# Stick-breaking attention with keys swept upwards: the factor of the later key blocks is applied after the value product, and the scores are computed four steps ahead

## The chip, the cores and the metric

The kernel runs on one core of one Trainium2 chip. The metric is the device time of one execution in microseconds (us), lower is better. The engines are named as the profile names them: PE is TensorE's matrix multiply and PEld its weight load, DVE is VectorE, ACT is ScalarE, POOL is GpSimd, SP is SyncE, which issues most transfers. Each engine runs its own instructions in the order in which the program gives them, and waits on semaphores for the others.

## The reference

A two-layer decoder trunk of width 1024 over 1024 tokens, all in float32. The part that the change touches is the stick-breaking attention of the first layer: eight heads of width 64, strictly causal.

```
def block(args):                       # one block of 128 queries
    z = jnp.einsum('bhqd,bhkd->bhqk', q_i, k) * scale
    mask = kpos[None, :] < qpos[:, None]
    log_fail = jnp.where(mask, jax.nn.log_sigmoid(-z), 0.0)
    later = lax.cumsum(log_fail, axis=3, reverse=True) - log_fail
    a = jnp.where(mask, jnp.exp(jax.nn.log_sigmoid(z) + later), 0.0)
    return jnp.einsum('bhqk,bhkd->bhqd', a, v)
```

So a key's weight is sigmoid(z) times the product of (1 - sigmoid(z)) over the keys between it and the query: each weight needs a sum over all *later* keys of the row. With sp = softplus(z) = max(z,0) + ln(1+exp(-|z|)), the weight is exp(z - sum of sp over this key and the later ones).

## The kernel before

The whole trunk is one program. Its stages follow each other: the first layer's projections with the gated delta rule, then stick-breaking attention, then the output projection, feed-forward, and the second layer. The time is spent above all in matrix products in which each float32 factor is split into two parts of the format fp32r ("hi" and "lo") and three of the four partial products are formed (`mm3`, lines 156 to 158).

Stick-breaking is the stretch of the program from line 899 to line 1066, and only it and the preparation of its operands are touched. The eight heads are taken as four pairs (`p` = 0 to 3). Within a pair a *step* is one block of 128 keys (`kb`) against one block of 256 queries (`i`), both heads of the pair at once, so most tiles are 128 keys by 2x256 queries, written 128x512. A pair has 20 steps, the four pairs 80. Two query blocks are always interleaved, (3, then 0) with (2, then 1). In 4 of a pair's 20 steps the key block reaches beyond half of the queries; such a half step works on the second half alone (128x2x128, which the profile writes 128x256). Before the change the keys of a query block run downwards, from the last block to block 0.

The pipeline of a step has these pieces, each a letter of the string `SORDER`, which sets the order in which the loop over n (line 1025) issues them; `Z+3` means "piece Z of step n+3", and because the loop is recorded by hand (`manual_schedule`), the engines run exactly this order:

- Z, lines 918 to 921, PE: the scores z = k·q, the key in parts kh and kl, plus a mask matmul of 128 columns where the block meets the diagonal. Two PSUM banks for z.
- A, E, L, lines 926, 929 and 932, ACT: ab = ln(1+exp(-|z|)) in three activations.
- K, line 936, DVE: a copy ls of z from PSUM to SBUF, which sets z's bank free.
- M, line 939, DVE: ab = max(ls,0) + ab, the softplus.
- h, line 945, DVE, and l, line 948, POOL: ab is split into sh and sl.
- Q, lines 959 and 960, PE: the negated sum over the keys of this block that are not earlier (`nstr` holds minus ones in a triangle) is added into a bank `Pb` that lives through all steps of the query block.
- W, line 963, DVE: ls = ls + Pb. X, line 1022, ACT: ls = exp(ls), the finished weights.
- C, lines 971 and 972, PE: the rest of the triangle (`ncom`) is added, so that Pb then holds the sum over the whole block for the blocks that follow. Left out in the last step of a query block.
- V, line 981, PE: weights times values, a plain float32 product, accumulated over the steps in the bank `av`, which ACT copies to `ob` (line 983) after the last step.

Three tokens bring in other work: `p` advances the preparation of the next pair's q and k (`prep_qk`: loads, a cast on ACT, a subtraction on POOL; `PREPS` says in which of the 20 steps which half of which operand starts), and `f` fills PE with matmuls that have nothing to do with the step: up to step 8 the last value projection (`v_gen`), and from step 18 on 64 units of three matmuls of the output projection (`out_gen`, lines 156 to 158, tile `ops`), about one unit a step. Every fourth unit needs an evacuation on DVE (line 304, below also "evac"), every sixteenth a new weight tile: a cast `whi` on ACT (line 141) and a subtraction `wlo` on DVE (line 142). In steps 13, 15, 17 and 19 the loop also splits four tiles of the delta rule's output into `o` (cast on ACT, line 1037, subtraction on DVE, line 1038), ahead of the step's own pieces. `VSHARE`, `OSPLIT`, `OSTART` and the rest of these numbers are the same in both kernels, and so is every instruction outside the stretch but for line numbers and the load of the constants `scr`.

Of the kernel before, what the change touches and what calls it, by code (L numbers as in the profile page):

```python
# [10 lines left out]
F32 = mybir.dt.float32  # L11
F32R = mybir.dt.float32r
AF = mybir.ActivationFunctionType
# [10 lines left out]
PREPS = {3: (0, 1), 6: (1, 1), 10: (0, 0), 15: (1, 0)}  # L24
SORDER = "Z+3 V-4 f Q+0 A+3 W+0 K+3 X-1 E+3 p p h+2 L+3 f C-1 l+2 M+3".split()
LSB, ABB, SHB = 8, 4, 3
# [35 lines left out]
def tile_trunk(ctx: ExitStack, tc: tile.TileContext, xT, cT, adaS, adaT, vec, w_ab, w_hyb, w_hout, w_rin, w_rout,  # L62
# [460 lines left out]
    def stack(tag, nm, p, half):  # L523
        i = 2 * p + 1 - half
        return (sqs[0] if i % 3 else sb0).tile([P, HT], F32R, tag=tag, name=nm, bufs=2 if i % 3 else 1)

    def prep_qk(p, isq, half, new, dma=None):

        src = qk_d[2 * p + isq][:, half * HT:half * HT + HT]
        dma = dma or nc.sync.dma_start  # L530
        if not isq:
            xs_ = []
            for h in range(2):
                x = new()
                for r in range(2):
                    dma(x[r * 64:r * 64 + 64], src[h * 64:h * 64 + 64])
                xs_.append(x)
            yield
            for h in range(2):
                kh = stacks[p, "kh", h, half] = stack(f"kh{h}", f"kh{p}{h}", p, half)  # L540
                kl = stacks[p, "kl", h, half] = stack(f"kl{h}", f"kl{p}{h}", p, half)
                A.copy(kh, xs_[h])
                yield
                G.tensor_tensor(kl, xs_[h], kh.bitcast(F32), op=ALU.subtract)
                yield
            return
        x = new()
        dma(x, src)
        yield
        ts = []  # L550
        for h in range(2):
            o = slice(h * 64, h * 64 + 64)
            qs = stacks[p, "q", h, half] = stack(f"q{h}", f"q{p}{h}", p, half)
            A.copy(qs[o], x[o])
            ts.append(qs)
            yield
        for h in range(2):
            o = slice(h * 64, h * 64 + 64)
            r = slice(64 - h * 64, 128 - h * 64)
            G.tensor_tensor(ts[h][r], x[o], ts[h].bitcast(F32)[o], op=ALU.subtract)  # L560
            yield

    def s_first():

        scr = sb0.tile([P, 4, P], F32R, tag="scr", name="scr")
        G.dma_start(scr[:, 0:3, :], cst[:, C_NSTR:C_NSTR + 3, :])
        V.tensor_copy(scr[:, 3, :], ident)
        scrs.append(scr)
        for isq in range(2):
            for _ in prep_qk(0, isq, 1, half_tile):  # L570
                pass
# [326 lines left out]
    with ExitStack() as sx:  # L898
        pz = sx.enter_context(tc.tile_pool(name="pz", bufs=2, space=PSUM))
        pP = sx.enter_context(tc.tile_pool(name="pP", bufs=1, space=PSUM))  # L900
        pav = sx.enter_context(tc.tile_pool(name="pav", bufs=1, space=PSUM))
        steps = []
        for p in range(4):
            two = [[dict(p=p, i=i, kb=kb, x=x, first=(kb == 2 * i + 1), last=(kb == 0), c0=128 if kb == 2 * i + 1 else 0)
                    for i in ii for kb in range(2 * i + 1, -1, -1)] for x, ii in enumerate(((3, 0), (2, 1)))]
            for pair in zip(*two):
                steps.extend(pair)
        cur = {}
        fin = []
# [13 lines left out]

        def stage_a(s):
            s["ab"] = ab = sp_.tile([P, HT], F32, tag="ab", name="ab", bufs=ABB).rearrange("p (h n) -> p h n", h=2)[:, :, s["c0"]:]
            A.activation(ab, s["z"], AF.Abs)
# [7 lines left out]
        def stage_k(s):  # L934
            s["ls"] = ls = sp_.tile([P, HT], F32, tag="ls", name="ls", bufs=LSB).rearrange("p (h n) -> p h n", h=2)[:, :, s["c0"]:]
            V.tensor_copy(ls, s["z"])

        def stage_sp(s):
            V.scalar_tensor_tensor(s["ab"], s["ls"], 0.0, s["ab"], op0=ALU.max, op1=ALU.add)

        def stage_hi(s):
            c0 = s["c0"]
            s["sh"] = sp_.tile([P, 2, 256], F32R, tag="sh", name="sh", bufs=SHB)[:, :, c0:]
            s["sl"] = sp_.tile([P, 2, 256], F32R, tag="sl", name="sl", bufs=SHB)[:, :, c0:]
            V.tensor_copy(s["sh"], s["ab"])
# [4 lines left out]
        def stage_h(s):  # L950
            stage_hi(s)
            stage_lo(s)

        def stage_t1(s):
            c0 = s["c0"]
            if s["first"]:
                cur["P", s["x"]] = pP.tile([P, 2, 256], F32, tag=f"P{s['x']}", name="Pb")
            s["P"] = Pc = cur["P", s["x"]][:, :, c0:]
            PE.matmul(Pc, nstr, s["sh"], start=s["first"], stop=False, skip_group_check=True)
            PE.matmul(Pc, nstr, s["sl"], start=False, stop=True, skip_group_check=True)  # L960

        def stage_t2(s):
            V.tensor_tensor(s["ls"], s["ls"], s["P"], op=ALU.add)

        def stage_t(s):
            stage_t1(s)
            stage_t2(s)

        def stage_c(s):
            if not s["last"]:  # L970
                PE.matmul(s["P"], ncom, s["sh"], start=False, stop=False, skip_group_check=True)
                PE.matmul(s["P"], ncom, s["sl"], start=False, stop=True, skip_group_check=True)

        def stage_av(s):
            p, i, kb, c0 = s["p"], s["i"], s["kb"], s["c0"]
            if s["first"]:
                cur["av", s["x"]] = pav.tile([P, 256], F32, tag=f"av{s['x']}", name="av")
            av = cur["av", s["x"]]
            for h in range(2):
                o = slice(h * 64, h * 64 + 64)  # L980
                PE.matmul(av[o, c0:], vts[p][:, kb, o], s["ls"][:, h, :], start=s["first"], stop=True, skip_group_check=True)
            if s["last"]:
                fin.append(lambda: A.copy(obt[p][:, i * 256:i * 256 + 256], av))
# [5 lines left out]
        nstr, ncom, negm, idr = (scrs[0][:, i, :] for i in range(4))  # L989
# [8 lines left out]
        with tc.manual_schedule(engines=COMPUTE):  # L998
# [3 lines left out]
            prep = [prep_qk(0, 0, 0, new_x, QD(nc)), prep_qk(0, 1, 0, new_x, QD(nc))]  # L1002
# [18 lines left out]
            def stage_x(s):  # L1021
                A.activation(s["ls"], s["ls"], AF.Exp)
            ops = dict(Z=stage_z, A=stage_a, E=stage_e, L=stage_l, K=stage_k, H=stage_h, T=stage_t, X=stage_x, C=stage_c, V=stage_av)
            ops.update(M=stage_sp, h=stage_hi, l=stage_lo, Q=stage_t1, W=stage_t2)
            for n in range(-6, 88):
# [22 lines left out]
                for f in fin:  # L1048
                    f()
                fin.clear()  # L1050
# [12 lines left out]
            for f in fin:  # L1063
                f()
# [830 lines left out]
```

## Time and profile before

| what | us |
|---|---|
| median of 3 runs | 3126.43 (3126.11 to 3132.8) |
| the profiled execution | 3130.16 |
| its span, first to last instruction | 3128.4 |
| granted TensorE clock, mean over the span | 0.991 |
| first softplus piece L of the stage (line 932) starts at | 620.5 |
| last of them starts at | 843.2 |
| last X of the stage (line 1022) starts at | 850.6 |
| first matmul of the output projection that reads `ob` | 854.64 |

The views used below are the windows (busy time of each engine in a stretch, with the mean granted TensorE clock and the share of the DMA engines), the groups (busy time and mean nanoseconds of one instruction for each line, engine and shape, and what ended the idle time ahead of them) and the timeline (start, duration, engine, line; in brackets how long the engine had been idle and who released it). A matmul's record is longer than the slot it takes, because matmuls overlap in the array: what a matmul costs PE is read from the start of one to the start of the next.

### The profile page before, as it was taken

The numbers are of one execution on the slowest core, as the hardware profiler recorded it, in microseconds if no ns is written. First come the engines' busy times: TensorE is split into PE (matmuls) and PEld (weight loads), VectorE is DVE, ScalarE is ACT, GpSimd is POOL, SyncE is SP. The second block draws the span as 40 slices with busy tenths as digits, with TensorE's granted clock in tenths as the row PEclk, the third lists the DMA queues.
The fourth block names the chain that finished last, engine by engine and source line by source line (L and its number), as shares of the span: only waits on it lengthen the run. The fifth ranks groups of instructions, "written<-read, shape, count | busy, mean of one in ns | idle before, by whom it ended". The sixth has DMA issues, their size and how long they took to land.

```text
span 3128.4 us, 38622 instructions
## 1 busy us (share of the span) xinstructions
PE 3008.5 (96%) x14616; PEld 2418.5 (77%) x14616; DVE 2118.7 (68%) x3065; ACT 1244.5 (40%) x2011; POOL 460.6 (15%) x332
## 2 busy tenths in 40 slices
PE   6999999999999999999999999999999899999999
PEld 3777788867677888887878788887777688888887
DVE  5778876599877655588582455578866976656445
ACT  4444556688763322221263332333223632223111
POOL 0233332077531000000040000001111300000000
PEclk8999999999999999999999999999999999999999
DMA  5333332241034322287125333362312342224222
GB/s 210 129 109 102 121 112 79 96 148 48 21 103 146 105 81 81 83 318 276 60 88 157 109 115 111 109 236 98 110 48 68 125 150 90 81 81 169 88 75 101
DMA packets 136602, 362.35 MB, mean 116 GB/s; under 512 B 15072, under 2 KB 24032, under 8 KB 135904
## 3 DMA queue, kind: packets, MB, share of 16 engines
q1 hardware_dynamic: 135808, 358.90, 34.3%
q8 instruction: 115, 1.88, 0.3%
q10 hardware_dynamic: 464, 0.79, 0.1%
q14 instruction: 71, 0.58, 0.1%
q0 software_dynamic: 144, 0.20, 0.0%
HBM read 282.76 MB, written 77.07 MB: 115 GB/s over the span
## 4 chain that ended last, share of the span: by engine, by line
PE 43%; DVE 8%; DMA 3%; issue 1%; ACT 1%; SPq 0%; DVEq 0%; ACTq 0%
PE ops L156 5%; PE ops L157 5%; PE ops L158 5%; PE rvps L1570 3%; PE mB L1271 2%; PE mB L1269 2%; PE mB L1270 2%; PE mD L1270 2%; PE mD L1269 2%; PE mD L1271 2%; PE mA L1269 2%; PE mA L1271 2%; PE mA L1270 2%; DMA adaw<-in_adaT_dram 1%; PE mE L1269 1%
## 5 line engine op out<-in xcount | busy, mean ns | idle before, releaser
L304 DVE SCALAR_TENSOR_TENSOR x<-ops,mod,x 128x512 f32<-128x512 f32 x288 | 215.3, 748 | 215.6 <-PE ops L158 215.1
L141 ACT CAST whi<-raw 128x1024 fp32r<-128x1024 f32 x158 | 165.5, 1051 | 398.7 <-PE ops L157 306.3
L156 PE MATMUL ops<-hdh,whi 128*128 128x512 f32 x704 | 276.4, 393 | 6.7 <-DVE x L304 6.3
L142 DVE TENSOR_TENSOR wlo<-raw,whi 128x1024 fp32r<-128x1024 f32 x158 | 208.1, 1319 | 101.1 <-ACT whi L141 96.5
L157 PE MATMUL ops<-hdl,whi 128*128 128x512 f32 x704 | 274.6, 390 | 0.0
L158 PE MATMUL ops<-hdh,wlo 128*128 128x512 f32 x704 | 274.1, 389 | 0.0
L156 PE MATMUL gps<-hh,whi 128*128 128x512 f32 x352 | 166.1, 472 | 0.0
L156 PEld LDWEIGHTS ops<-hdh,whi 128*128 128x128 f32 x704 | 132.1, 188 | 42.3 <-DVE x L304 12.3
L158 PEld LDWEIGHTS ops<-hdh,wlo 128*128 128x128 f32 x704 | 132.2, 188 | 27.9 <-issue 0.2
L157 PEld LDWEIGHTS ops<-hdl,whi 128*128 128x128 f32 x704 | 132.2, 188 | 26.9 <-issue 0.2
L192 POOL TENSOR_TENSOR nscr<-nscr 128x512 f32<-128x512 f32 x30 | 46.2, 1541 | 691.5 <-ACT nscr L191 633.6
L1261 ACT CAST thi<-raw 128x512 fp32r<-128x512 f32 x180 | 101.8, 618 | 114.4 <-DVE raw L1257 68.9
L157 PE MATMUL gps<-hl,whi 128*128 128x512 f32 x352 | 140.8, 400 | 0.0
L158 PE MATMUL gps<-hh,wlo 128*128 128x512 f32 x352 | 139.7, 397 | 0.0
L156 PE MATMUL ops<-osh,whi 128*128 128x512 f32 x320 | 128.3, 406 | 10.1 <-DVE x L304 8.1
L948 POOL TENSOR_TENSOR sl<-ab,sh 128x512 fp32r<-128x512 f32 (+1 forms) x80 | 116.4, 1455 | 140.6 <-ACT ab L932 73.8
L157 PE MATMUL ops<-osl,whi 128*128 128x512 f32 x320 | 128.1, 401 | 5.3 <-DVE osl L1749 4.8
L158 PE MATMUL ops<-osh,wlo 128*128 128x512 f32 x320 | 126.1, 395 | 0.0
L1262 DVE TENSOR_TENSOR tlo<-raw,thi 128x512 fp32r<-128x512 f32 x180 | 119.3, 710 | 3.3 <-ACT thi L1261 3.3
L1400 ACT ACTIVATE u<-u 128x512 f32<-128x512 f32 x44 | 27.8, 632 | 231.1 <-DVE u L1331 231.1
L1331 DVE TENSOR_TENSOR u<-u,mE 128x512 f32<-128x512 f32 x60 | 41.3, 688 | 112.2 <-PE mE L1271 112.2
L1311 DVE TENSOR_TENSOR u<-u,mB 128x512 f32<-128x512 f32 x60 | 41.3, 688 | 111.6 <-issue 100.1
(425 smaller groups left out, 8445.1 us busy)
## 6 DMA issues: line engine op xcount, KB each, us to landing
raw<-in_w_fin_dram SPq DMA_DIRECT2D x102, 512.0 KB, 3.8
raw<-in_w_rin_dram SPq DMA_DIRECT2D x64, 512.0 KB, 4.0
raw<-in_w_fout_dram SPq DMA_DIRECT2D x52, 512.0 KB, 3.6
adaw<-in_adaT_dram SPq DMA_DIRECT2D x48, 512.0 KB, 4.9
oraw<-hid_d SPq DMA_DIRECT2D x44, 512.0 KB, 5.3
gth<-in_adaT_dram SPq DMA_DIRECT2D x64, 256.0 KB, 2.8
raw<-in_w_hyb_dram SPq DMA_DIRECT2D x28, 512.0 KB, 3.6
hid_d<-c SPq DMA_DIRECT2D x44, 256.0 KB, 2.0
```

The source lines that it names most:

```text
L141: A.copy(hi, raw)
L142: V.tensor_tensor(lo, raw, hi.bitcast(F32), op=ALU.subtract)
L156: PE.matmul(ps, whi, xh, start=start, stop=False)
L157: PE.matmul(ps, whi, xl, start=False, stop=False)
L158: PE.matmul(ps, wlo, xh, start=False, stop=stop)
L304: V.scalar_tensor_tensor(xs[dt][:, sl], ps, gts(dt), xs[dt][:, sl], op0=ALU.mult, op1=ALU.add)
L948: G.tensor_tensor(s["sl"], s["ab"], s["sh"].bitcast(F32), op=ALU.subtract)
L1261: A.copy(hi, t)
L1262: e.tensor_tensor(lo, t, f32(hi), op=ALU.subtract)
L1269: PE.matmul(ps, w[0][:, c], xh[k], start=(start and k == 0), stop=False, skip_group_check=True)
L1270: PE.matmul(ps, w[0][:, c], xl[k], start=False, stop=False, skip_group_check=True)
L1271: PE.matmul(ps, w[1][:, c], xh[k], start=False, stop=(k == 3), skip_group_check=True)
```

## The change

The keys of a query block now run upwards, from block 0 to the diagonal. A step forms weights that hold only the sum over its *own* block, multiplies them with the values at once, and the result of the earlier steps is multiplied by the factor of the new block, because this block's keys are all later than theirs: acc = acc * exp(-sum of sp over this block) + weights·v. The accumulator is now `ob` in SBUF instead of a PSUM bank.

- Z moves to the end of the step and one step further ahead (`Z+4`), and z keeps its PSUM bank until X has read it; there are four banks for z.
- A of a full step is now a bit operation on DVE that clears the sign (line 930, from PSUM); only half steps keep ACT's Abs.
- K is gone; M reads z from PSUM.
- Q adds the triangle onto z itself, so W is gone, and X reads z in PSUM.
- C is replaced by S: four matmuls with a matrix of ones (`som`) that lay the sums of sp over the block, for both heads, into the second half of the new bank `av` (two banks, taken in turn), left out in the first step of a query block instead of the last.
- G is new, on ACT: g = exp(-sum), 128 partitions by 256 queries. R is new, on POOL: acc = acc * g. O is new, on DVE: acc = acc + av, or a copy in the first step. The four copies of `av` for each pair on ACT are gone.
- V runs one step behind instead of four.
- PREPS changes which halves are prepared when, and `stack` chooses the buffers accordingly; `scr` has three constants instead of four and is loaded by two transfers instead of one.

```
-SORDER = "Z+3 V-4 f Q+0 A+3 W+0 K+3 X-1 E+3 p p h+2 L+3 f C-1 l+2 M+3".split()
-LSB, ABB, SHB = 8, 4, 3
+PREPS = {3: (0, 0), 6: (1, 1), 15: (1, 0), 18: (0, 1)}
+SORDER = "A+3 Q+0 S+0 X+0 V-1 M+2 E+3 f h+2 R-1 L+3 p G+0 f l+2 O-1 Z+4 p".split()
+WB, ABB, SHB = 3, 4, 3
...
-        pz = sx.enter_context(tc.tile_pool(name="pz", bufs=2, space=PSUM))
-        pP = sx.enter_context(tc.tile_pool(name="pP", bufs=1, space=PSUM))
-        pav = sx.enter_context(tc.tile_pool(name="pav", bufs=1, space=PSUM))
+        pz = sx.enter_context(tc.tile_pool(name="pz", bufs=4, space=PSUM))
+        pav = sx.enter_context(tc.tile_pool(name="pav", bufs=2, space=PSUM))
...
+            if s["c0"]:
+                A.activation(ab, s["z"], AF.Abs)
+            else:
+                V.tensor_scalar(ab.bitcast(I32), s["z"].bitcast(I32), 0x7FFFFFFF, None, op0=ALU.bitwise_and)
...
-        def stage_k(s):
-            s["ls"] = ls = sp_.tile([P, HT], F32, tag="ls", name="ls", bufs=LSB).rearrange("p (h n) -> p h n", h=2)[:, :, s["c0"]:]
-            V.tensor_copy(ls, s["z"])
...
-            V.scalar_tensor_tensor(s["ab"], s["ls"], 0.0, s["ab"], op0=ALU.max, op1=ALU.add)
+            V.scalar_tensor_tensor(s["ab"], s["z"], 0.0, s["ab"], op0=ALU.max, op1=ALU.add)
...
-            V.tensor_tensor(s["ls"], s["ls"], s["P"], op=ALU.add)
...
+        def stage_q(s):
+
+            PE.matmul(s["z"], nstr, s["sh"], start=False, stop=False, skip_group_check=True)
+            PE.matmul(s["z"], nstr, s["sl"], start=False, stop=True, skip_group_check=True)
+
+        def stage_x(s):
+            s["w"] = half2(sp_.tile([P, HT], F32, tag="w", name="w", bufs=WB), s)
+            A.activation(s["w"], s["z"], AF.Exp)
+
+        def stage_s(s):
+
+            s["av"] = av = pav.tile([P, 2, 256], F32, tag="av", name="av")
             if s["first"]:
+                return
+            for h in range(2):
+                e = som[:, 64 - 64 * h:192 - 64 * h]
+                for j, t in enumerate((s["sh"], s["sl"])):
+                    PE.matmul(av[:, 1, s["c0"]:], e, t[:, h, :], start=(h + j == 0), stop=(h + j == 2), skip_group_check=True)
+
+        def stage_g(s):
+            if not s["first"]:
+                s["g"] = g = sp_.tile([P, 256], F32, tag="g", name="g", bufs=3)
+                A.activation(g[:, s["c0"]:], s["av"][:, 1, s["c0"]:], AF.Exp, scale=-1.0)
...
+                PE.matmul(s["av"][o, 0, c0:], vts[p][:, kb, o], s["w"][:, h, :], start=True, stop=True, skip_group_check=True)
...
+            if not s["first"]:
+                G.tensor_tensor(acc(s), acc(s), s["g"][:, s["c0"]:], op=ALU.mult)
+
+        def stage_o(s):
+            av = s["av"][:, 0, s["c0"]:]
+            if s["first"]:
+                V.tensor_copy(acc(s), av)
+            else:
+                V.tensor_tensor(acc(s), acc(s), av, op=ALU.add)
```

Two places show what the string makes of the engines' orders. A row names the line, the operation, the written tile and the read ones, and in brackets the engines whose semaphores it waits for.

The first is PE in a full step of the steady part of the stage. Before, the step begins with Q (lines 959, 960), then come C of the step ahead of it, Z, V and a unit of `f`:

```order
L959 MATMUL Pb<-sh,scr 128x512 [waits DVE_49]
L960 MATMUL Pb<-sl,scr 128x512 [waits Pool_49]
L971 MATMUL Pb<-sh,scr 128x512 [waits DVE_49]
L972 MATMUL Pb<-sl,scr 128x512
L918 MATMUL z<-q_5767,kh_5917 128x256 [waits DVE_49,PE_49]
L919 MATMUL z<-q_5767,kl_5918 128x256
L918 MATMUL z<-q_5805,kh_5945 128x256
L919 MATMUL z<-q_5805,kl_5946 128x256
L981 MATMUL av<-ls,vt_5659 64x128 [waits Activation_49]
L981 MATMUL av<-ls,vt_5659 64x128
```

The same place now, with Q (951, 952), S (966), V of the step before (977), the unit of `f`, and Z (917 on):

```order
L951 MATMUL z<-sh,scr 128x512
L952 MATMUL z<-sl,scr 128x512 [waits Pool_49]
L966 MATMUL av<-sh,som 128x256 [waits DVE_49]
L966 MATMUL av<-sl,som 128x256
L966 MATMUL av<-sh,som 128x256
L966 MATMUL av<-sl,som 128x256
L977 MATMUL av<-w,vt_6398 64x256 [waits Activation_49]
L977 MATMUL av<-w,vt_6398 64x256
L157 MATMUL ops<-o_6147,whi 128x512
L158 MATMUL ops<-o_6148,whi 128x512
L159 MATMUL ops<-o_6147,wlo 128x512
L917 MATMUL z<-q_6507,kh_6923 128x256 [waits Activation_49]
```

The wait that C had on DVE (W of the step before must have read Pb) has become S's wait on DVE: its bank `av` is the one that O of two steps before reads, and O of two steps before stands in DVE's order one loop step earlier, as the last of that step. Z's wait on DVE has become a wait on ACT (X of the same loop step).

The second place is DVE in a step in which a weight tile of the output projection is split (`wlo`). Before, `wlo` and the evacuation (line 304) stand at the start of the step, ahead of W, K, h and M:

```order
L939 SCALAR_TENSOR_TENSOR ab<-ls,ab 128x512 [waits DVE_49,Activation_49]
L142 TENSOR_TENSOR wlo<-raw,whi 128x1024 [waits DMAHW0_49,Activation_49]
L304 SCALAR_TENSOR_TENSOR x_5880<-ops,mod,x_5880 128x512
L963 TENSOR_TENSOR ls<-ls,Pb 128x512 [waits PE_49]
L936 COPY ls<-z 128x2x128 [waits Activation_49]
```

Now they stand inside the step, behind A (930) and M (940), ahead of h (944) and O (991):

```order
L930 TENSOR_SCALAR ab<-z 128x512 [waits PE_49]
L940 SCALAR_TENSOR_TENSOR ab<-z,ab 128x512 [waits Activation_49]
L143 TENSOR_TENSOR wlo<-raw,whi 128x1024 [waits DMAHW5_49,Activation_49]
L305 SCALAR_TENSOR_TENSOR x_5917<-ops,mod,x_5917 128x512
L944 CAST sh<-ab 128x512 [waits DVE_49]
L991 TENSOR_TENSOR ob_5321<-ob_5321,av 128x256 [waits PE_49,Pool_49]
```

A's wait on PE is for Z, the last piece of the PE step before, and `wlo`'s wait on ACT is for the cast `whi`, which now stands on ACT behind X and E of the same step. What is queued behind `wlo` is h and O, and S of the next step waits for O.

More of the change, by code (lines that the diff above doesn't have):

```diff
@@ L521, in load_v, with stack @@
         nc.sync.dma_start(vts[p], v_d[:, :, p * P:p * P + P])
[L523 to L524 removed]
+    def stack(tag, nm, p, half, isq):
+        i = 2 * p + (1 - half if isq else half)
         return (sqs[0] if i % 3 else sb0).tile([P, HT], F32R, tag=tag, name=nm, bufs=2 if i % 3 else 1)
@@ L988, in tile_trunk @@
         sp_ = sx.enter_context(tc.tile_pool(name="sbp", bufs=2, side="right"))
-        nstr, ncom, negm, idr = (scrs[0][:, i, :] for i in range(4))
+        nstr, negm, idr = (scrs[0][:, i, :] for i in range(3))
+        som = sp_.tile([P, 192], F32R, tag="som", name="som", bufs=1)
+        for i in range(3):
+            V.tensor_scalar(som[:, 64 * i:64 * i + 64], ones[:, 0:64], float(i == 1), None, op0=ALU.mult)
         xs = []
```

73 lines of the change are left out of this document (21 added, 52 removed).

## The prediction, made before the changed kernel was run

> **What bounds the kernel now.** I read the page first, then the windows over the stage, then the timeline of one steady step, and the groups for the prices. The page:
>
> ```profile
> PE 3008.5 (96%) x14616; PEld 2418.5 (77%) x14616; DVE 2118.7 (68%) x3065; ACT 1244.5 (40%) x2011; POOL 460.6 (15%) x332
> ```
>
> PE is busy nearly always, but that is an average over all stages, so it is read again for the stage alone (columns: window, its us, busy time and instructions of PE, PEld, DVE, ACT and POOL, the granted clock, the DMA share, GB/s).
>
> ```profile
> 656.60:695.30 38.70, 33.47 (x183) 22.66 (x182) 38.06 (x60) 34.12 (x68) 23.77 (x18) 0.96 0.40 133
> 695.30:849.20 153.90, 152.38 (x849) 110.34 (x848) 144.68 (x238) 127.85 (x248) 103.82 (x72) 1.00 0.12 37
> 849.20:855.90 6.70, 4.76 (x27) 2.51 (x26) 3.94 (x5) 4.68 (x7) 0.00 (x0) 0.99 0.13 27
> 852.00:855.70 3.70, 1.96 (x14) 0.85 (x10) 2.87 (x3) 3.44 (x6) 0.00 (x0) 1.00 0.20 32
> 855.70:859.10 3.40, 3.20 (x8) 2.53 (x9) 3.40 (x4) 1.73 (x2) 0.00 (x0) 0.51 0.31 124
> ```
>
> The first window is steps 10 to 22, in which the `o` splits stand, the second the steady steps 23 to 78, the third the tail from the last Q to the second matmul of the next stage. In the second PE and DVE both look full, 152.4 and 144.7 of 153.9 us. Which of the two sets the pace is read from starts:
>
> ```profile
> 706.35 0.40 PE L959 MATMUL Pb<-sh,scr 128*128 128x512 f32 x1
> ...
> 706.82 0.40 PE L971 MATMUL Pb<-sh,scr 128*128 128x512 f32 x1
> ...
> 707.29 0.28 PE L918 MATMUL z<-q,kh 128*128 128x256 f32 x1
> ...
> 707.85 0.65 PE L981 MATMUL av<-ls,vt 128*64 128x256 f32 x4
> 708.43 0.50 PE L156 MATMUL ops<-o,whi 128*128 128x512 f32 x1
> ...
> 709.23 0.40 PE L959 MATMUL Pb<-sh,scr 128*128 128x512 f32 x1
> ```
>
> Start to start, Q takes 0.47 us, C 0.47, Z 0.56, V 0.58, a unit of f 0.80: 2.88 us a step without a gap. PE's slots bound the steady stage, and DVE, 94% busy, is a near second. Where PE does wait, it is at `wlo`:
>
> ```profile
> 725.90 2.31 DVE L142 TENSOR_TENSOR wlo<-raw,whi 128x1024 fp32r<-128x1024 f32 x1
> 729.32 0.39 PE L960 MATMUL Pb<-sl,scr 128*128 128x512 f32 x1
> ...
> 730.22 0.36 PE L918 MATMUL z<-q,kh 128*128 128x256 f32 x1 [0.50 <-DVE ls L936]
> ```
>
> 730.22 is Z kept 0.50 us by K. The 153.9 us hold some 1.7 us of such waits in all: where `wlo` delays DVE by 2.31 us, PE loses about half a microsecond, since W, K and M then work a step or more ahead of what PE needs.
>
> **The change part by part: PE's slots.** Q, Z, V and f stay. S in a full step is four matmuls of 256 columns, C two of 512: 0.47 us either way. In a half step C's two take
>
> ```profile
> 726.73 0.28 PE L971 MATMUL Pb<-sh,scr 128*128 128x256 f32 x1
> 726.85 0.29 PE L972 MATMUL Pb<-sl,scr 128*128 128x256 f32 x1
> ```
>
> 0.12 us each by starts, 0.24 together; S's four of 128 columns lie between half of that each (0.24, nothing lost) and the same 0.12 each (0.48): 0 to +0.24 us. No row shows four such ones; I take +0.2, near the upper end, since four weight loads stay four. Twelve half steps lie outside the first window: **+2.4 us**. V one step behind instead of four only moves three V (3 x 0.58 = 1.7) from behind the last Q to before it: **+1.7**, which the tail gives back.
>
> **DVE's prices.** Groups of the steady window (busy us, mean ns, idle before):
>
> ```profile
> L939 DVE SCALAR_TENSOR_TENSOR ab<-ls,ab 128x512 f32<-128x512 f32 x45 | 39.8, 885 | 0.8 <-ACT ab L932 0.7
> L963 DVE TENSOR_TENSOR ls<-ls,Pb 128x512 f32<-128x512 f32 x46 | 31.3, 681 | 6.7 <-PE Pb L960 6.4
> L936 DVE COPY ls<-z 128x512 f32<-128x512 f32 x44 | 30.0, 682 | 0.0
> L945 DVE CAST sh<-ab 128x512 fp32r<-128x512 f32 x45 | 22.9, 509 | 0.0
> L304 DVE SCALAR_TENSOR_TENSOR x<-ops,mod,x 128x512 f32<-128x512 f32 x14 | 10.4, 741 | 0.0
> L142 DVE TENSOR_TENSOR wlo<-raw,whi 128x1024 fp32r<-128x1024 f32 x4 | 9.3, 2318 | 0.0
> L963 DVE TENSOR_TENSOR ls<-ls,Pb 128x256 f32<-128x256 f32 x10 | 4.2, 418 | 0.7 <-PE Pb L960 0.5
> ```
>
> Before, a full step costs DVE W 0.68, K 0.68, h 0.51, M 0.89: 2.76 us. W and K go. A as a bit operation on z is not in the trace: bounds are h's 0.51 (same elements, from SBUF) and M's 0.89; I take K's 0.68, the same shape out of PSUM. M now reads z in PSUM, like W: 0.68 instead of 0.89 (bounds 0.68 and 0.89). O has the shape of the half-step W, 0.42 (bounds 0.42 and, by M's price per element, 0.45). Sum 2.29, so 0.47 us a step fall away on DVE.
>
> But the order takes more than that. S(n) waits for O(n-2), the *last* DVE instruction of the step before, while A, the *first* one, waits for Z at the end of the PE step before that. So one whole DVE step must fit between Z's end and the next step's S. Setting 0 at the Q of a 2.88 us step: Z's result is there 0.20 us later (the last Q, 849.44 below, has a slot of 0.24, and W starts 0.44 after its start), A ends at 0.88, M 1.56, h 2.07, O 2.49. S of the next step stands at 2.88 + 0.47 = 3.35: cover 0.8 us. Behind S on PE stand V, f and Z, so a late O stops everything.
>
> - *Evacuation* (0.74, row L304), now between M and h, just fits; in shorter steps of 2.4 to 2.6 us it misses by up to 0.4. Two or three of 14: **+0.8**.
> - *`wlo`*. Its cast `whi` now stands on ACT behind X and E:
>
> ```profile
> L1022 ACT ACTIVATE ls<-ls 128x512 f32<-128x512 f32 x47 | 29.4, 626 | 8.3 <-DVE ls L963 8.3
> L926 ACT ACTIVATE ab<-z 128x512 f32<-128x512 f32 x43 | 25.6, 595 | 13.0 <-PE z L919 7.1 <-PE z L921 5.7
> L141 ACT CAST whi<-raw 128x1024 fp32r<-128x1024 f32 x4 | 4.1, 1032 | 0.0
> L983 ACT COPY ob<-av 128x256 f32<-128x256 f32 x11 | 3.9, 355 | 0.0
> ```
>
> X starts at 0.67 and ends at 1.30, E 1.93, whi 2.96; then wlo 1.23 (alone, row 852.67 below) to 4.23, evacuation 4.97, h 5.48, O 5.90, S at 6.0 instead of 3.35: a wait of **2.65 us**. Beside POOL, wlo took 2.32, which would give 3.7; with its whi done before, 1.2. I take 2.65, as POOL too runs dry while h waits. Three of the four are of this kind, one (without an evacuation, whi ahead of E) gives 1.3: 3 x 2.65 + 1.3 = 9.2, less the 1.7 of before: **+7.5 us**.
> - *`o` splits*. DVE pays 2.29 at the head of a step,
>
> ```profile
> 664.90 2.29 DVE L1038 TENSOR_TENSOR o<-x,o 128x1024 fp32r<-128x1024 f32 x1
> ```
>
> then its 2.29 of A, M, h, O: 4.58 against 2.08 + 0.47 = 2.55 in a step without f, so S waits 2.0, four times, and one `wlo` lies there too: 8 + 2.65 = 10.7. Before: PE's slots in the 38.7 us are some 28 us (ten steps of 2.1, two with f), so it waited 10.7 there as well. **0.**
>
> **ACT and POOL.** ACT loses A (0.60) and the `ob` copies and gains G (0.36 by row L983, same shape out of PSUM; bounds 0.3 and 0.42): less work, no cost. Z(n+4) waits for X(n), done at 1.30, Z stands at 2.41: cover 1.1 us.
>
> ```profile
> L948 POOL TENSOR_TENSOR sl<-ab,sh 128x512 fp32r<-128x512 f32 x46 | 72.1, 1567 | 36.1 <-DVE sh L945 26.0 <-PE Pb L959 4.0 <-PE Pb L972 3.2
> L948 POOL TENSOR_TENSOR sl<-ab,sh 128x256 fp32r<-128x256 f32 x10 | 10.1, 1014 | 13.3 <-DVE sh L945 9.9 <-PE ops L158 3.4
> L544 POOL TENSOR_TENSOR kl<-sx,kh 128x512 fp32r<-128x512 f32 x8 | 11.0, 1377 | 0.0
> L560 POOL TENSOR_TENSOR q<-sx,q 64x512 fp32r<-64x512 f32 x8 | 11.3, 1408 | 0.6
> ```
>
> POOL gains R, 1.01 by the second row (bounds 0.78, half of a full sl, and 1.57). A plain step is then 1.57 + 1.01 = 2.6 of 2.88. In a step with a preparation (1.4), sl, kl and R make 4.0: R ends late, O behind it. POOL catches up 0.3 a step; I take **+1.0 us** for all 24 (0 to 7). What else changes (three small writes of `som`, one more transfer of constants) lies before the stage beside its fills: nothing; uncovered, under 1 us.
>
> **The tail.**
>
> ```profile
> 849.21 0.39 PE L959 MATMUL Pb<-sh,scr 128*128 128x512 f32 x1
> 849.44 0.40 PE L960 MATMUL Pb<-sl,scr 128*128 128x512 f32 x1
> 849.88 0.69 DVE L963 TENSOR_TENSOR ls<-ls,Pb 128x512 f32<-128x512 f32 x1 [1.72 <-PE Pb L960]
> ...
> 852.67 1.23 DVE L142 TENSOR_TENSOR wlo<-raw,whi 128x1024 fp32r<-128x1024 f32 x1
> ...
> 854.64 0.73 PE L156 MATMUL ops<-osh,whi 128*128 128x512 f32 x2 [1.42 <-ACT osh L1496]
> 855.90 0.80 PE L157 MATMUL ops<-osl,whi 128*128 128x512 f32 x1 [0.53 <-DVE osl L1497]
> ```
>
> Before 6.7 us from the last Q to the `osl` matmul. After: Q to result 0.67, X 0.63, V 0.3 + 0.2, O 0.3, the cast of `ob` 1.05, its subtraction 1.2, steps between engines 0.25: 4.6, **-2.1** (bounds 0 and -3). The clock then fell to 0.51 for 3.4 us (855.70 to 859.10) after 3.7 us in which PE was busy for 1.96; a shorter gap may spare that, half of 3.2 us: **-1.6**. The same rows warn of the `wlo` waits: 2.65 us of idle PE is more than the 1.7 missing there, and may halve the clock once or twice at 1.7 us each: **+2** (0 to +5).
>
> The Trainium skill, "TensorE: Matmul & The Clock Gate", section "HAM oscillation — how this bites in real kernels", puts the limit at idle gaps of over some 3.4 us; by it the waits here would cost nothing more, and the sum would be 2 us lower. The row of 855.70 fell after a gap of half that length, and I go by the row.
>
> **Sum:** 2.4 + 1.7 + 0.8 + 7.5 + 0 + 1.0 - 2.1 - 1.6 + 2 = +11.7 us on the profiled execution, 3130.2 (span 3128.4). That one lies 3.7 above the median of 3126.4, and all terms are differences: 3126.4 + 11.7 = **3138 us**.
>
> **Rivals.**
> - *(B) The order gives enough cover*, as DVE's 0.47 us less a step and four z banks let M, h and O catch up. For it: DVE is shorter in every step; against it: A cannot start before Z. Then `wlo` costs nothing (-1.7), the first window shrinks by about its clock dip and half its waits (-4.6), tail and clock -3.7, half steps 0 to +2.4, V +1.7: -8 to -6, **3118 to 3121**.
> - *(C) POOL becomes the bound* (slower still). A pair then costs it 16 x 1.57 + 4 x 1.01 (sl) + 12 x 1.01 + 4 x 0.6 (R) + 8 x 1.39 (preparation) = 54.7 us, against some 55 us of PE a pair: it decides as soon as R costs over 1.05, since R holds O and O holds S. At 1.3, 12 x 0.3 = 3.6 a pair over three pairs, on top of part of the sum: **3143 to 3150**.
> - *(D) DVE was the bound*, PE's full rows being stalls that its records hide. Then 47 x 0.47 = 22 us go, less what S and V add: **3104 to 3110**. Against it stand starts 2.88 apart without a gap. The Trainium skill, "Trainium Kernel Development and Optimization", section "Performance Expectations", calls matmul busy time a bad metric and weight-load busy share a good one. Here that share is 110 of 154 us, 72%, which speaks for (D); the starts decide against it.
> - *(E) It washes out*: `wlo` waits of 1.2 each by an early whi (-4), no clock dips (-2): 3126 to 3132.
>
> **How the numbers follow.** A measurement of this kernel tells about 0.2%, 6.3 us, from no change: faster is under 3120.2, slower over 3132.7. The forecast's case 0.50 (its bounds 3133 to 3145); B 0.22, half of it below 3120.2; C 0.09; D 0.07; E 0.12. Faster 0.11 + 0.07 = 0.18; same 0.11 + 0.12 = 0.23; slower 0.59. The range takes in all but D and the edges: 3116 to 3152; the forecast's own is 3133 to 3145.
>
> **What would show it.** Q starts 2.88 us apart in plain steps and about 5.5 where `wlo` stands, with S idle there behind DVE's O: right. M near 690 ns and R near 1.0 us: the prices. From the last Q to the `osl` matmul 4.6 us, and the clock at 1.00 behind it: the tail. Wrong: no idle ahead of S (B), S idle behind O and O behind R in plain steps (C), Q starts under 2.8 apart in steps with f (D).

## The result, and the profile after

| | kernel before | changed kernel |
|---|---|---|
| median, us | 3129.6 (4 runs, 3126.1 to 3135.0) | 3150.0 (4 runs, 3148.4 to 3152.0) |
| ratio | | 1.0064, 95% interval 1.0046 to 1.0082 |
| the profiled execution, us (span) | 3130.2 (3128.4) | 3148.9 (3147.0) |

The change makes the kernel slower, by some 20 us where 11.7 were forecast. The page of the changed kernel hardly shows it: PE is still at 96%, and DVE has lost 32 us of work without any gain in time.

```profile
PE 3022.9 (96%) x14744; PEld 2430.8 (77%) x14744; DVE 2086.5 (66%) x3052; ACT 1228.0 (39%) x1995; POOL 483.0 (15%) x397
```

So the stage is cut at the same places in both traces: at one matmul ahead of the stage that is the same in both, at the starts of the first, 14th, 24th and last Q, and at the first matmul that reads `osl`. The second trace of the kernel before is one of the runs below.

| stretch, us | before | before, second trace | changed | difference |
|---|---|---|---|---|
| fixed matmul to first Q | 31.6 | 31.6 | 30.0 | -1.6 |
| Q of steps 0 to 13 | 36.5 | 36.6 | 39.6 | +3.1 |
| Q of steps 13 to 23 | 32.2 | 32.2 | 34.2 | +2.0 |
| Q of steps 23 to 79 (last) | 153.9 | 153.9 | 168.2 | +14.3 |
| last Q to the `osl` matmul | 6.7 | 6.7 | 7.3 | +0.6 |
| sum | 260.9 | 261.0 | 279.3 | +18.4 |

Nearly the whole loss lies in the stage, and three quarters of it in the steady steps, where PE had been almost without a gap. The windows over the first `o` splits, the steady steps and the tail of the changed kernel (same columns as before the change):

```profile
657.80:696.27 38.47, 32.36 (x177) 22.86 (x177) 29.73 (x52) 29.08 (x59) 24.41 (x24) 0.87 0.40 124
696.27:864.52 168.25, 161.92 (x951) 118.51 (x949) 122.86 (x227) 117.84 (x243) 118.10 (x119) 0.97 0.10 31
864.52:871.00 6.48, 4.63 (x26) 2.87 (x24) 2.93 (x5) 3.34 (x5) 0.46 (x1) 1.00 0.00 1
```

Two things differ in the steady row: PE is idle for 6.3 us where it was idle for 1.5, and the granted clock is 0.97 where it was 1.00. DVE's busy time fell from 144.7 us in 153.9 to 122.9 in 168.3. What PE waits for, by the view of the waits for PE in that window (waiting line, engine and line waited for, us in all, times, the longest):

```profile
PE av L966 <- DVE ob L991: 4.5, 5, 1.8
PE av L966 <- DVE ob L989: 1.7, 1, 1.7
```

L966 is S, L991 and L989 are O: every wait of PE in the steady steps is S waiting for O. One of the three long ones, in time order over the engines, in the step whose Q starts at 826.66 (the next Q at 829.58):

```profile
827.37 0.60 ACT L956 ACTIVATE w<-z 128x512 f32<-128x512 f32 x1 [1.04 <-PE z L952]
827.86 0.62 ACT L933 ACTIVATE ab<-ab 128x512 f32<-128x512 f32 x1
828.38 1.04 ACT L142 CAST whi<-raw 128x1024 fp32r<-128x1024 f32 x1
```

```profile
829.45 1.22 DVE L143 TENSOR_TENSOR wlo<-raw,whi 128x1024 fp32r<-128x1024 f32 x1 [1.30 <-ACT whi L142]
830.59 0.74 DVE L305 SCALAR_TENSOR_TENSOR x<-ops,mod,x 128x512 f32<-128x512 f32 x1
831.25 0.42 DVE L944 CAST sh<-ab 128x512 fp32r<-128x512 f32 x1
831.59 0.41 DVE L991 TENSOR_TENSOR ob<-ob,av 128x256 f32<-128x256 f32 x1
```

```profile
829.82 0.40 PE L952 MATMUL z<-sl,scr 128*128 128x512 f32 x1
832.05 0.38 PE L966 MATMUL av<-sh,som 128*128 128x256 f32 x1 [1.84 <-DVE ob L991]
```

X, E, `whi`, then `wlo`, the evacuation, h, O, and 0.05 us after O's end S: the chain of the prediction, link by link. The bracket on L143 shows that DVE itself stood idle for 1.30 us until `whi` was done.

The second loss is the clock. These windows are 3.41 us long or twice that, and end where the granted clock changes (third number from the right):

```profile
731.66:735.07 3.41, 1.68 (x12) 0.94 (x10) 3.38 (x6) 2.26 (x7) 1.27 (x2) 1.00 0.33 98
735.07:741.90 6.83, 6.83 (x23) 4.85 (x22) 2.05 (x5) 2.95 (x7) 5.48 (x7) 0.50 0.08 30
782.85:786.26 3.41, 1.77 (x11) 1.22 (x12) 2.92 (x6) 1.38 (x5) 2.01 (x2) 1.00 0.53 159
```

```profile
786.26:789.67 3.41, 3.41 (x16) 2.85 (x14) 1.74 (x4) 1.09 (x2) 2.20 (x4) 0.50 0.00 0
666.80:677.03 10.23, 10.23 (x38) 7.17 (x39) 6.32 (x11) 8.00 (x17) 7.07 (x8) 0.50 0.26 84
```

Behind two of the three long waits PE ran at half clock, for 6.83 and 3.41 us; if half of that is lost, as it is where PE has no other wait, this makes 5.1 us. Around the `o` splits it ran so for 10.23 us, at most 5.1 lost, where the kernel before lost at most 1.7 (3.4 us at half clock, from 668.0). PE looks fully busy in all these windows: a busy share doesn't show a slow clock.

The prices on DVE and POOL, from the groups of the steady window:

```profile
L940 DVE SCALAR_TENSOR_TENSOR ab<-z,ab 128x512 f32<-128x512 f32 x43 | 29.3, 681 | 0.0
L930 DVE TENSOR_SCALAR ab<-z 128x512 int32<-128x512 int32 x42 | 29.0, 690 | 19.4 <-PE z L918 11.7 <-PE z L920 7.6
L944 DVE CAST sh<-ab 128x512 fp32r<-128x512 f32 x44 | 27.3, 621 | 1.0
L991 DVE TENSOR_TENSOR ob<-ob,av 128x256 f32<-128x256 f32 x36 | 14.9, 415 | 16.2 <-POOL ob L984 10.2 <-PE av L977 6.0
```

```profile
L947 POOL TENSOR_TENSOR sl<-ab,sh 128x512 fp32r<-128x512 f32 x44 | 56.9, 1293 | 38.5 <-DVE sh L944 35.9 <-PE z L952 1.6 <-ACT ab L936 0.9
L984 POOL TENSOR_TENSOR ob<-ob,g 128x256 f32<-128x256 f32 x36 | 27.3, 758 | 2.5 <-ACT g L971 2.2
```

A (690 ns), M (681) and O (415) cost what was forecast; h is dearer (621 for 510 ns) and R cheaper (758 ns for 1.01 us). O's idle time says what holds O in a plain step: R on POOL, more often than V.

### The profile page after: what moved, and what is told of

It is laid out like the page before. It is cut to its first block, busy times and chain, and to the rows that moved or that the text cites. A ratio compares the mean times of both kernels' runs of the same rounds, so it can differ in the third digit from the quotient of the medians.

```text
span 3147.0 us, 38793 instructions
## 1 busy us (share of the span) xinstructions
PE 3022.9 (96%) x14744; PEld 2430.8 (77%) x14744; DVE 2086.5 (66%) x3052; ACT 1228.0 (39%) x1995; POOL 483.0 (15%) x397
## 4 chain that ended last, share of the span: by engine, by line
PE 71%; DVE 15%; DMA 5%; ACT 4%; issue 3%; POOL 1%; SPq 0%; DVEq 0%; ACTq 0%; POOLq 0%
PE ops L157 6%; PE ops L158 5%; PE ops L159 5%; PE rvps L1575 4%; PE mB L1276 3%; PE mB L1274 3%; PE mB L1275 3%; PE mD L1275 3%; PE mD L1274 3%; PE mD L1276 3%; PE mA L1274 3%; PE mA L1276 3%; PE mA L1275 3%; DMA adaw<-in_adaT_dram 2%; PE mE L1276 2%
## 5 line engine op out<-in xcount | busy, mean ns | idle before, releaser
L143 DVE TENSOR_TENSOR wlo<-raw,whi 128x1024 fp32r<-128x1024 f32 x158 | 202.9, 1285 | 108.2 <-ACT whi L142 103.7
L947 POOL TENSOR_TENSOR sl<-ab,sh 128x512 fp32r<-128x512 f32 (+1 forms) x80 | 94.3, 1179 | 137.1 <-ACT ab L936 75.1
```

The source lines that it names most:

```text
L143: V.tensor_tensor(lo, raw, hi.bitcast(F32), op=ALU.subtract)
```

## The experiments

The orders quoted are the string `SORDER`; the changed kernel has "A+3 Q+0 S+0 X+0 V-1 M+2 E+3 f h+2 R-1 L+3 p G+0 f l+2 O-1 Z+4 p". "The stage" below is from the fixed matmul ahead of it to one that is the same in all, half a microsecond to one behind the `osl` matmul: 261.9 us before (262.0 in the second trace), 280.3 changed. Of each version but the kernel before there is one trace.

**The two orders that give S more time.**

```diff
+SORDER = "A+3 Q+0 X+0 V-1 M+2 E+3 f h+2 R-1 L+3 p S+0 G+0 f l+2 O-1 Z+4 p".split()
```

> Edit: on PE, S stands behind V and the unit of f instead of right behind Q; nothing else moves but G's place on ACT. Theory T1 (S waits for O of two steps before, which a late DVE step delays; the wait, and the halved clock it sets off, make the loss): S stands 1.4 us later in a step with f (V 0.58, f 0.80), so the waits of 1.9 to 2.0 us where wlo stands fall to about 0.5 and those of 0.5 behind an evacuation to nothing; the two stretches of half clock in the steady stage (10.2 us, 5.1 us lost) are gone. Time 3133 to 3140. Theory T2 (the loss is PE's own slots: four small matmuls in S, V earlier): no change, 3148 to 3152.

```diff
+SORDER = "A+3 Q+0 f S+0 X+0 V-1 M+2 E+3 h+2 R-1 L+3 p G+0 f l+2 O-1 Z+4 p".split()
```

> Edit: the unit of f stands between Q and S on PE; with it whi stands ahead of X on ACT, and wlo and the evacuation between A and M on DVE. T1: S stands 0.8 us later (1.6 in the early steps), whi is ready about 1.9 us earlier, O ends about 4.6 us after the step's start where wlo stands, S is at 4.15: waits of about 0.5 us instead of 2, no half clock in the steady stage. Time 3134 to 3142. T2: no change, 3148 to 3152. If the order of S and f alone counts (not whi's place), it lies between the changed kernel and the one with S behind f.

S behind f: 3144.4 us, ratio 1.0043 (1.0028 to 1.0058); the stage 271.7 us. f ahead of S: 3141.5, 1.0034 (1.0022 to 1.0045); 269.5. The waits for O shrank, in the first of them to those below, where V now waits a little for G on ACT; with f ahead of S one wait of 1.0 us for O is left, where about 0.5 was expected.

```profile
PE av L977 <- ACT g L971: 1.2, 4, 0.4
PE av L966 <- DVE ob L991: 0.5, 2, 0.2
PE av L966 <- DVE ob L989: 0.4, 1, 0.4
```

The granted clock is 1.00 over the steady steps in both; the first has

```profile
697.80:857.50 159.70, 157.34 (x950) 110.75 (x949) 124.09 (x226) 120.88 (x242) 117.02 (x118) 1.00 0.11 32
```

So about half of the loss was S's wait and the clock behind it: 8.6 and 10.8 us of 18.4 are won back by moving S or f alone. "No change" is refuted. But the median with S behind f came out above the range given, and both stay over the kernel before: something else costs 8 to 10 us. In the steady steps it is hardly waiting, as the row shows: PE is busy for 157.3 us of them, where it was busy for 152.4 in the kernel before. The theory that PE's own slots cost more holds for this part. That f ahead of S is no slower than S behind f hints that the earlier place of `whi` counts too, but the two intervals overlap, so this stays open.

**How much room O has.** Two additions that nobody reads, ahead of O:

```diff
         def stage_o(s):
+            for _ in range(2):
+                V.tensor_tensor(sp_.tile([P, 256], F32, tag="dm", name="dm", bufs=2), ones256, ones256, op=ALU.add)
```

> Edit: two additions of 128x256 that nobody reads stand ahead of O on DVE in every step, 0.4 us each by the price of O. T1: DVE's cover in a plain step with f is about 0.8 us, so plain steps with f grow by 0 to 0.2 us, steps without f (2.4 us) by 0.5 or more, steps with an evacuation by 0.8, steps with wlo by 0.8 each: 25 to 50 us more in all, and S idles behind O in most steps. T2 (PE's slots bound, DVE has room): under 3 us more.

```profile
L988 DVE TENSOR_TENSOR dm<-o 128x256 f32<-128x256 f32 x115 | 98.5, 896 | 0.0
```

3215.4 us in its one run, 65 more than the changed kernel where 25 to 50 was expected; first to last Q 304.5 us instead of 242.0. The dose was twice what was meant: an addition of two SBUF operands took 0.90 us here, where O, with one operand in PSUM, takes 0.41. Plain steps with f, at full clock, grew by 0.8 to 0.9 us (step 24: 3.77 instead of 2.89) for 1.77 of dose by starts, so DVE had some 0.9 us of room ahead of S; the prediction had 0.8. A rise in DVE's work by 1.8 us a step costs nearly a microsecond in such steps; a step without S, such as step 41, didn't grow (2.41 us in both).

**POOL.** R's two lines are left out, so that the accumulator isn't multiplied.

> Left out: R, so that the accumulator isn't multiplied by the later block's factor (G is still computed). T1: POOL is beside the path, O waits for V and not for R; h and wlo may get a little shorter without POOL beside them; 0 to 4 us less. Theory T3 (POOL's R holds O, and O holds S): S's waits in plain steps and behind the preparations go, 6 us or more less.

3143.2 in one run; the stage 276.0, 4.3 less, which lies between the 0 to 4 of the one theory and the 6 or more of the other. The three long waits for O stay, 5.5 us in all, with the half clock behind them:

```profile
PE av L966 <- DVE ob L990: 3.7, 2, 1.9
PE av L966 <- DVE ob L988: 1.8, 1, 1.8
```

Only the three short waits went, 0.9 us in all by this view; two of them stood where a preparation kept R late. 2.0 of the 4.3 us are in steps 13 to 23. That POOL sets the time is refuted, since the long waits stand without R; R costs a little.

**The half steps.** In a half step S is two matmuls of 256 columns against a full matrix of ones.

```diff
+            if s["c0"]:
+                PE.matmul(av[:, 1, :], one, s["sh"], start=True, stop=False, skip_group_check=True)
+                PE.matmul(av[:, 1, :], one, s["sl"], start=False, stop=True, skip_group_check=True)
+                return
```

> Edit on the changed kernel: in the 16 half steps S is two matmuls of 256 columns against a full matrix of ones (both heads' sums side by side) instead of four of 128; G of a half step becomes two activations of 64 partitions. T2 in part (the half steps' S costs PE more than the 0.2 us of the prediction; by the pieces of the trace 0.27): PE's slots fall by some 0.25 x 16 = 4 us, all waits of S stay: first to last Q 237 to 240 instead of 242. If waits take up what slots give (O sets S in every step): first to last Q stays at 241 to 243.

First to last Q 238.6 us, 3.4 less, where 2 to 5 less was expected; but the number proves little. By the starts, S in a half step fell from 0.485 to 0.325 us, 16 x 0.16 = 2.6, but in this trace half clock also lasted 3.4 us in the steady steps instead of 10.2, which alone is 3.4 us; and steps 13 to 23 took 1.2 us more, with longer waits. With the clock out of the way (last run below), the steady steps gain only 0.8.

**O ahead of h.** Meant to take h's and `wlo`'s place away from O; *combo* adds the half steps' S and moves the `o` splits to the first f.

```diff
+SORDER = "A+3 Q+0 f X+0 V-1 S+0 M+2 E+3 R-1 O-1 h+2 l+2 L+3 p G+0 f Z+4 p".split()
```

> Edit on the changed kernel: PE's order is Q f V S f Z, and O and R stand ahead of h, so that neither wlo nor the evacuation of a later step stands between M and O, whi stands ahead of X, and S stands 1.4 us later. T1: no wait of S over 0.3 us in the steady stage, no half clock there, first to last Q 229 to 231. The first window (o splits at the head of a step) keeps most of its waits. Time 3133 to 3140, what is left against the kernel before being PE's slots and the tail. If the waits were set by DVE's total work and not by its order: waits of Q on sl in their place, no gain over f ahead of S (first to last Q 231.5).

> Edit: o_first, with the half steps' S as in shalf, and the o splits moved from the head of the step to the first f. If the loss consisted of waits, half clock and half-step slots, first to last Q comes to 222 to 227, near the 222.6 of the kernel before, and the time to 3128 to 3135. If something else is in it, it stays at 228 or more and the time over 3135.

Both missed widely: 3160.0 (1.0096, 1.0078 to 1.0113) and 3158.1 (1.0085, 1.0064 to 1.0106), and from first to last Q 251.6 and 250.0 us against the changed kernel's 242.0. The steady waits of the first, its two largest rows:

```profile
PE av L966 <- DVE ob L991: 4.8, 10, 0.8
PE z L952 <- POOL sl L947: 4.4, 11, 0.9
```

No wait is long, but there are many, also in plain steps. O now waits for R behind POOL's preparation, h stands behind O, sl behind h, and Q waits for sl:

```profile
714.92 1.29 POOL L545 TENSOR_TENSOR kl<-sx,kh 128x512 fp32r<-128x512 f32 x1
716.17 0.72 POOL L984 TENSOR_TENSOR ob<-ob,g 128x256 f32<-128x256 f32 x1
717.86 1.29 POOL L947 TENSOR_TENSOR sl<-ab,sh 128x512 fp32r<-128x512 f32 x1 [0.96 <-DVE sh L944]
```

```profile
716.93 0.42 DVE L991 TENSOR_TENSOR ob<-ob,av 128x256 f32<-128x256 f32 x1 [1.57 <-POOL ob L984]
717.27 0.42 DVE L944 CAST sh<-ab 128x512 fp32r<-128x512 f32 x1
```

DVE idles 1.57 us until R ends at 716.89, and POOL then idles 0.96 until h ends. The changed order, h ahead of O, keeps POOL fed while O waits.

**A second trace of the kernel before.**

> The kernel before, unchanged, for a second trace of it: how much of the difference outside the stage (2.5 us less ahead of it, 3.2 us more behind it in the changed kernel's trace) is there between two traces of one kernel. If it is chance: ahead of the stage and behind it the two traces of before differ by 2 us or more; if it belongs to the change: they agree within 0.5 us.

The stage agrees to 0.1 us (the table above). Ahead of it the two traces differ by 0.5 us, behind the `osl` matmul by 2.0 (2272.4 and 2274.4 us to the end). The changed kernel's 2.5 us less ahead of the stage lies beyond that, while of the 2.8 more behind that matmul (2275.2) two traces of one kernel can differ by 2.0; no experiment looked further into either.

**`wlo` alone.** `wlo`, and with it the load of the next weight tile, is issued one unit of f, about a step, later; the order is the changed one.

```diff
-                V.tensor_tensor(lo, raw, hi.bitcast(F32), op=ALU.subtract)
+                if deferred:
+                    later(2, lambda: (V.tensor_tensor(lo, raw, hi.bitcast(F32), op=ALU.subtract), w_load()))
+                else:
+                    V.tensor_tensor(lo, raw, hi.bitcast(F32), op=ALU.subtract)
```

> Edit on the changed kernel: the subtraction wlo is issued one unit of f (about one step) behind its cast whi, so that it stands neither behind whi on ACT nor together with an evacuation in one step; SORDER as changed. T1: with whi done long before, O ends at 2.49 + 1.23 = 3.7 against S at 3.35: waits of 0.4 to 0.8 us in place of 1.9 at the three places, too short to halve the clock: first to last Q 242 less 3 x 1.3 less 5.1 = 233. If wlo alone sets the wait (not whi and the evacuation ahead of it): 238 or more.

3137.8 us, 1.0032 (1.0020 to 1.0045); first to last Q 231.0, 11.0 less, the stage 268.9. The steady window and all of PE's waits in it:

```profile
695.50:853.20 157.70, 156.82 (x950) 115.09 (x949) 123.20 (x227) 117.44 (x243) 120.68 (x119) 1.00 0.11 33
```

```profile
PE av L970 <- DVE ob L995: 0.7, 2, 0.4
```

A few instructions, each moved by a step, undo 11.4 of the 18.4 us. The long waits were three things in one step: `whi` late behind X and E, `wlo`, and the evacuation. `wlo` by itself, with `whi` ready, fits into O's room.

**Together.** First f ahead of S with the half steps' S, the later `wlo` and the `o` splits at the first f; then, in the changed order, the half steps' S, the later `wlo` and the `o` splits in eight halves, one a step, at the first f.

> Edit: f ahead of S (as in f_before_s), the half steps' S as in shalf, wlo one unit later, the o splits at the first f of their step; O stays behind h, as changed. Each edit by its own run: f_before_s 231.5 from first to last Q, less 3.5 (shalf), less 2 (wlo), less 0 to 2 (o splits): 224 to 227; time 3131 to 3137. If POOL or DVE is full by then (as where O stood ahead of h): 229 or more.

> Edit on the changed kernel, SORDER as changed: wlo one unit later, the half steps' S as in shalf, and the o splits in eight halves of 128x512, one a step from step 13 to 20, behind M and E and ahead of h, instead of four whole ones at the head of every second step. T1: the two edits give 231 - 3.5 = 227.5 from first to last Q; with halves of 0.7 to 1.2 us on DVE a step, O is late by at most some 0.5 where it was by 2, and the 10 steps 13 to 23 shrink from 33.7 to 29 to 32 with no half clock: first to last Q 222.5 to 226, time 3127 to 3134, level with the kernel before or a little below. If DVE and POOL are full in these steps whatever the pieces: 227 or more, and 3132 to 3138.

3136.3 (1.0022, 1.0011 to 1.0033), first to last Q 228.6, between the two ranges given; and 3137.0 (1.0027, 1.0018 to 1.0037), 230.0, in the range for DVE and POOL being full. But in the steady steps it is PE that is full:

```profile
695.00:851.91 156.91, 155.76 (x929) 112.53 (x927) 124.19 (x228) 120.59 (x254) 120.63 (x119) 1.00 0.11 33
```

This is the second of the two versions: PE idles there for 1.2 us of 156.9, and DVE and POOL for over 30. The stage comes to 266.5 and 267.7, not to 261.9; the gains of the single edits don't add up. Smaller `o` splits gained nothing: steps 13 to 23 take 33.5 us, and one stretch of 3.4 us at half clock is still there. No version found beats the kernel before.

## Why the prediction was right, and what was mis-sized

Direction and cause held: slower, and S's waits for O with the clock behind them make more than half of the loss. The size was too small, +11.7 us for +20.4. The 3150 measured lies within the wide range, 3116 to 3152, which had to take in the rivals, but above the forecast's own bounds, 3133 to 3145; that it falls at the edge of rival C's 3143 to 3150 is chance, as the run without R shows. By its steps:

- **PE's slots bound the kernel before; S waits for O.** Right: every steady wait is S behind O, and moving S, f or `wlo` takes most of it away. That DVE was the bound (D) is refuted: DVE's busy time fell by 22 us and the steady steps grew. That the order gives enough cover (B) is refuted by the rows at 829.45 to 832.05, and that it washes out (E) by the time.
- **Cover 0.8 us.** Right; some 0.9 by the dose.
- **`wlo`, +7.5.** Right mechanism, too large: three waits of 1.9 to 2.0 us by starts and one of 0.4, 6.2 less the 1.7 of before, **+4.5**. Durations were added where starts should have been: in the quoted step `wlo` lasts 1.22 but the evacuation starts 1.14 later, and that record of 0.74 and h's of 0.42 keep the next one back by 0.66 and 0.34. O ended 5.34 us after the step's Q, not 5.90.
- **The clock, +2 and -1.6.** The mis-sized term, and the largest part of the missing 8.7 us. Measured: 5.1 us in the steady steps and up to 3.4 more around the `o` splits, **up to +8.5**, and nothing saved in the tail, behind which the clock fell again. Going by the row of 855.70 was right, since waits of 1.9 us by starts (1.7 in the view of waits) were enough. The Trainium skill, "TensorE: Matmul & The Clock Gate", section "HAM oscillation — how this bites in real kernels", has the rule that PE should have no idle gaps over some 3.4 us. This trace does not agree that shorter ones are safe, as the two waits of 1.7 us show. The step that failed is the count: the prediction took one or two stretches of 3.4 us in the steady steps (+2), where there were three such periods, and none at the `o` splits, where there were two more than before.
- **`o` splits, 0.** The stretch is 2.0 us longer: PE idles for 6.1 us in it instead of 5.2, up to 3.4 more are lost to the clock, and it holds one unit of f less (0.8 us). The prediction took 10.7 us of waits on both sides, although its own row for 656.60 to 695.30 has PE idle for 5.2; that the two cancelled was luck.
- **Half steps, +2.4.** Right, a little small: S takes 0.485 us there by starts where C took 0.24, so 0.245 each against the 0.2 taken, +2.9. But "0.47 us either way" in a full step is too small as well: S takes 0.56 there (median), of which the shorter Z behind it gives most back; plain steps are 2.92 us apart instead of 2.88.
- **V earlier, +1.7.** Right in kind: two V, not three, moved to before the last Q, +1.4 in steps 0 to 13. The +1.5 of the table's first two stretches agrees by chance, since they hold other things too (below).
- **Evacuation, +0.8.** Alone it delays nothing; two waits of 0.5 us by starts were POOL's, R behind a preparation: **POOL, +1.0**, right.
- **Tail, -2.1.** Wrong, +0.6. The step that failed is that the cast of `ob` follows O at once:

```profile
868.32 1.04 ACT L142 CAST whi<-raw 128x1024 fp32r<-128x1024 f32 x1 [2.64 <-PE ops L158]
869.27 3.88 ACT L1501 CAST osh<-ob 128x1024 fp32r<-128x1024 f32 x4
```

O ended at 867.34, but on ACT a `whi` stands ahead of the cast and waits for the last unit of f, which PE now runs behind the last V instead of ahead of it.

The steady steps can be summed by the two rows of windows. Of their 14.3 us, PE's longer idle time makes 4.8 (6.3 instead of 1.5) and the half clock 5.1. The other 4.4 are PE's own work, and this part stands alone in the run with `wlo` later: full clock, 0.9 us idle, and PE busy for 156.8 us where it was busy for 152.4 before. By starts it is S: 25.7 us in that run for the same number of steps in which C took 19.8, and Q and Z give 1.5 of it back. Ahead of them PE does not wait for anything in steps 0 to 13 of the changed kernel, and yet takes 3.1 us more (the kernel before first):

```profile
626.59:663.05 36.46, 36.10 (x244) 29.18 (x242) 32.73 (x51) 32.05 (x62) 31.40 (x23) 1.00 0.54 186
622.52:662.10 39.58, 39.58 (x285) 32.01 (x283) 28.61 (x50) 30.53 (x62) 34.03 (x32) 1.00 0.56 184
```

S takes 1.6 us more than C there, V 1.4, and two units of the value projection (0.9 us) have come from ahead of the first Q, where they are missing in the -1.6. So the loss is a little more than half waits and clock, as forecast in kind, and about a third PE's own slots, for which the forecast had too little. These slots are most of what the best versions keep.

## What to carry to other kernels

When a buffer's reader moves to the end of another engine's step, that whole step becomes the cover, and everything that is now and then slipped into it (a cast, a split, an evacuation) counts against it; look for steps in which several such pieces meet, and move one of them a step before rebuilding the order. Add up starts, not durations, along a chain on one engine. A wait on TensorE of two microseconds may cost as much again in clock: look at the granted clock of the windows behind each wait, since the busy share hides it. When the waits are gone and the time is still longer, compare PE's busy time at full clock: four small matmuls in the place of two large ones may cost more than they seem to.

## What the runs showed of the hardware

The clock changed on a fixed grid: in the changed kernel all half-clock stretches start whole multiples of 3.413 us apart (666.80, 735.07, 786.26), and in the stage they last one to three periods. In the stages of the kernel before and of the changed one, PE's busy time in a period tells what followed better than the longest single gap: periods at full clock with up to 1.83 of 3.41 us busy were each followed by a clock of 0.50, and those with 1.95 or more by 1.00, though PE's longest gap was 0.91 us in the first row below and 1.47 in the second. The first row is the kernel before, the others the changed one:

```profile
664.60:668.01 3.41, 1.83 (x9) 0.72 (x7) 3.41 (x5) 2.08 (x6) 1.51 (x1) 1.00 0.23 77
```

```profile
687.28:690.70 3.42, 1.95 (x13) 1.20 (x12) 3.35 (x7) 2.89 (x6) 2.99 (x4) 1.00 0.14 41
...
830.63:834.05 3.42, 2.00 (x11) 1.39 (x12) 3.42 (x7) 2.48 (x5) 1.98 (x2) 1.00 0.49 158
```

This is no threshold that can be carried elsewhere. With O ahead of h, in the same stage, it came out the other way round: the period at 658.65 was followed by 0.50, the one at 682.54 by 1.00.

```profile
658.65:662.06 3.41, 1.96 (x16) 1.47 (x16) 1.75 (x4) 1.21 (x4) 2.53 (x4) 1.00 0.98 367
682.54:685.95 3.41, 1.68 (x9) 1.20 (x9) 3.35 (x6) 1.50 (x4) 2.84 (x3) 1.00 0.27 54
```

In the kernel before, ahead of the stage, a period with 2.33 us busy (91.14) was followed by half clock and one with 1.62 (186.71) by full clock. What decides is not shown. The third long wait, of 2.0 us, cost no clock; the grid cut it in two (830.06 to 832.05, with a border at 830.63), which may be why. Why a stretch goes on for a second period with PE busy throughout, as at 735.07, stays open too.

DVE and POOL seem to trade time, though no run set this apart: as the subtraction sl on POOL fell from 1567 to 1293 ns, the cast h on DVE rose from 509 to 621. Without R on POOL h took 573, with sl unchanged at 1289. An addition from SBUF alone took 896 ns where one of the same size with an operand in PSUM took 408 in the same run.
